# v and u of twelve sample tiles as two blocks of Strassen products, in an encoder layer of 256 + 2048 tokens

## The chip, the cores and the metric

The kernel runs on one core of one Trainium2 chip. The metric is device time in microseconds (us) of one execution. The engines are TensorE (PE, with its weight loads PEld), VectorE (DVE), ScalarE (ACT), GpSimd (POOL) and SyncE (SP). All DMAs of this kernel are issued from SP's queue, in program order.

## The reference

One encoder layer in float32, applied to 256 prompt tokens and, separately, to 2048 sample tokens, with D = 1024.

```python
h = rms_norm(x, g_pre)
q, k, v, z_a, u_f, z_f = jnp.split(h @ w_in, ...)      # six parts of 512 columns
y_a = neighbourhood_attention(q, k, v, rpb)            # grid of 64 columns, 8 heads of 64,
                                                       # window 8 rows x 16 columns, softmax with bias
y_f = fourier_mix(u_f, w_fourier, b_fourier)           # real part of a 2-D FFT (tokens, 64 channels)
                                                       # per group, then a 512x512 product and a bias
mixed = concat([rms_norm(y_a, g_na) * silu(z_a), rms_norm(y_f, g_f) * silu(z_f)])
return x + rms_norm(mixed @ w_out, g_post)
```

## The kernel before

**Products.** Every fp32 product is made of three matmuls of parts in a reduced format (fp32r): an operand a is split in a high part ah (a cast, on ACT) and a low part al = a - ah (on DVE or POOL), and `mm3` adds ah bh, ah bl and al bh in PSUM. Its three lines, L160 to L162, hold most matmuls of the profile; a line there is told apart by its tiles.

**Direct stage (c loop).** Tokens are cut in tiles of 128: c = 0, 1 are the prompt, c = 2 to 17 the 16 sample tiles. For each tile `p_mm` makes v (128 x 512) and then u (128 x 512), 8 k-steps of `mm3` each, from the tile's split x (`x_split`; xh, xl) as stationary operand and the split weights with g_pre multiplied in (wc, `split_w`). The root-mean-square factor comes in when the result leaves PSUM (`v_out`, `u_out`, by invt). `x_square`, `pair_square` and `stats` make it: squares on ACT, sums over k by a reduction on DVE (sq), the sum over partitions by a matmul with ones on PE (pst, L295), then Ln, Exp and a correction. v goes to DRAM in 64 KB pieces (`vD`, with the columns that overlap written twice); each sample tile's u goes right away through the first Fourier step (`u_stage1`, three matmuls into pz), whose result goes to `ZD`. `wo_prep`, one step per tile from c = 8 to 16, loads w_out, splits it and stores it to `woD`.

**Prompt loop (b = 0 to 15).** z, k and q of the prompt, one product of 128 x 256 per step.

**Sample loop (i = 0 to 15).** z, k and q of the samples in Strassen-Winograd form: the k-dimension is halved, tokens are in two groups sg = 0, 1 of 1024 (i < 8 and i >= 8) with two blocks of 512 each, and each i makes two 128-row blocks of output by 7 products of 12 matmuls of 128 x 512. The token operands `bnew[sg, j]` (j = 0 to 6; xh, xl) are sums and differences of scaled x blocks: `n_load`, `n_scale` (x times g_pre times the scale of its token, `inv_all`), `n_sum` (DVE), `n_first` (split) for sg = 0; `n_diff`, `n_put` (to DRAM, `xD`), `b_get`, `b_split` for sg = 1. The weight operands (wa, aop) are made one i ahead: `w_load`, `w_sums` (sums on POOL, L440), `a_split` (ACT and DVE, L454 and L455). The bias tables of attention are made in between (`t_load`, `t_mask`, `t_store`).

**Rest.** Fourier's second stage, attention, output (`po`, L1257), from about 572 us of the span on.

**Order.** Each engine's instructions are in an order written by hand, which is that of the program text. The pool `gp` has 13 buffers of 512 KB (tag g), the pool `hp` 16 of 1 MB (tag k8); in PSUM the tag mm has 5 buffers, b 2, c 1. A tile of a pool waits for the last use of the buffer that it takes.

Of the kernel before, what the change touches and what calls it, by code (L numbers as in the profile page):

```python
# [34 lines left out]
XP = range(4, 17, 3)  # L35
# [88 lines left out]
def layout(inp):  # L124
# [4 lines left out]
    a["xs"] = x[TP:].reshape(32, 4, 16, KC, 128).transpose(2, 4, 3, 1, 0).reshape(16, 128, KC, 128)  # L129
# [3 lines left out]
    a["wv"], a["wu"] = [m.reshape(4, 2, 128, 512).transpose(0, 2, 1, 3) for m in (v, u)]  # L133
# [31 lines left out]
def build(tc, A, O):  # L165
# [13 lines left out]
    uD = dr.tile([TP, 512], F32, name="uD")  # L179
    xD = dr.tile([7, 128, 4, 512], F32, name="xD")  # L180
# [33 lines left out]
    inv_all = hp.tile([128, T], F32, name="inv_all")  # L214
    onesq = hp.tile([128, 128], F32, name="onesq")
    csm = hp.tile([128, 80], F32, name="csm")
    rmask = hp.tile([128, 48], F32, name="rmask")
    nc.gpsimd.memset(onesq, 1.0)
# [33 lines left out]
    def fold_u(raw):  # L252
        t = gt(US, F32, "uc")
# [6 lines left out]
        return t  # L260


    def xload(c):
        xs[c] = load(BS, A["xt"][c] if c < 2 else A["xs"][c - 2], "xr")

    def x_split(c, ks=slice(0, 8)):
        if c not in xh:
# [3 lines left out]
        (nc.gpsimd if c in XP else nc.vector).tensor_tensor(out=l, in0=xs[c][:, ks], in1=h.bitcast(F32),  # L271
                                                            op=ALU.subtract)

    def x_square(c):
        xr = xs.pop(c)
        nc.scalar.activation(xr, xr, AF.Square)
        if c % 2 == 0:
            sqs_[c] = st.tile([128, 256], F32, tag="sq", name="sq")
        nc.vector.tensor_reduce(out=sqs_[c - c % 2][:, c % 2 * 128:c % 2 * 128 + 128],  # L279
                                in_=xr.rearrange("p k t -> p t k"), axis=mybir.AxisListType.X, op=ALU.add)  # L280

    def pair_load(c):
        pr_[c] = k8(F32, "xx", (128, KC, 256))
        for x in range(2):
            nc.sync.dma_start(pr_[c][:, :, 128 * x:128 * x + 128], A["xs"][c - 2 + x])

    def pair_square(c):
        xr = pr_.pop(c)
        nc.scalar.activation(xr, xr, AF.Square)
        sqs_[c] = st.tile([128, 256], F32, tag="sq", name="sq")  # L290
        nc.vector.tensor_reduce(out=sqs_[c], in_=xr.rearrange("p k t -> p t k"), axis=mybir.AxisListType.X, op=ALU.add)

    def stats(c):
# [16 lines left out]
        if c == 0:  # L310
            nc.scalar.copy(inv_all[:, :TP], y)
# [31 lines left out]
    def u_out(g):  # L343
        p = acc.pop(("u", g))
        if pend:
            u_stage1(*pend.pop())
# [212 lines left out]
    for c in range(2):  # L559
        v_out(c)  # L560
# [1025 lines left out]
```

## Time and profile before

| | |
|---|---|
| runs | 1002.38, 1004.58, 1005.26 us; median 1004.58 |
| profiled execution | 1003.15 us, of which the span is 1001.2 us |
| granted TensorE clock, mean | 0.996 |
| matmuls | 5828 |
| bytes moved | 249.33 MB (read 160.13, written 88.08 by memory) |

Stages in the trace, in us of the span: direct stage 5 to 220, prompt loop 220 to 267, sample loop 267 to 572, the rest to 1001. A row of a group reads: line, engine, operation, out<-in, partitions x elements, count | busy us in all, mean ns of one | idle time of the engine before it, and what ended that. A row of the chain or of a timeline begins with start and duration in us. A row of the windows has, behind the stretch, its length and the busy time of PE, PEld, DVE, ACT and POOL with counts, then the granted clock, the DMA share and GB/s. A row of waits has the total, the number and the longest, in us.

### The profile page before, as it was taken

To read this page: it belongs to the slowest core of one execution; us is meant where nothing else is said; L and a number is where in the kernel's file an instruction comes from. 1 tells how busy PE (TensorE), PEld (TensorE's weight loads), DVE (VectorE), ACT (ScalarE), POOL (GpSimd) and SP (SyncE) were. 2 spreads that over 40 slices of the span, in tenths; PEclk is the share of its full clock that TensorE was granted. 3 is DMA by queue.
4 is the path that set the end of the run, shared out by engine and by line. 5 is a ranking of instruction groups with operands and counts; after the bars stand their busy time and mean duration, and the time that the engine had idled before them with its cause. 6 is when DMAs were issued, how large, how long until landed. Compare 5 with 4: busy or idle time off the path is not lost.

```text
span 1001.2 us, 16950 instructions
## 1 busy us (share of the span) xinstructions
PE 987.3 (99%) x5828; PEld 819.9 (82%) x5828; DVE 688.2 (69%) x1295; ACT 474.4 (47%) x1026; POOL 438.3 (44%) x401
## 2 busy tenths in 40 slices
PE   7999999999999999999999999999999999999997
PEld 6778888889988888888888879777787787888886
DVE  7777637668767788697666345776656565648997
ACT  6554424256533322432222255676666665734443
POOL 2300000100336476477657033477577686524444
PEclk9999999999999999999999999999999999999999
DMA  7467788877455685865764898588778799869993
GB/s 257 140 182 222 214 304 310 269 253 255 148 191 194 231 316 191 335 238 210 259 213 169 301 329 298 179 272 286 239 218 260 253 301 295 274 205 343 338 340 129
DMA packets 153253, 249.33 MB, mean 249 GB/s; under 512 B 14032, under 2 KB 99344, under 8 KB 150608
## 3 DMA queue, kind: packets, MB, share of 16 engines
q1 hardware_dynamic: 153168, 248.26, 73.3%
q8 instruction: 46, 0.75, 0.3%
q14 instruction: 39, 0.32, 0.1%
HBM read 160.13 MB, written 88.08 MB: 248 GB/s over the span
## 4 chain that ended last, share of the span: by engine, by line
PE 94%; DVE 2%; DMA 1%; ACT 1%; issue 1%; SPq 0%; POOL 0%; DVEq 0%; ACTq 0%; POOLq 0%
PE po L1257 19%; PE mm L161 17%; PE mm L160 17%; PE mm L162 17%; PE pv L1327 6%; PE ptb L1311 6%; PE s L1006 4%; PE pab L851 2%; DMA wr<-wv 1%; PE py L160 1%; PE py L162 1%; PE py L161 1%; DVE wc L248 1%; DVE sq L279 1%; PE pz L161 0%
## 5 line engine op out<-in xcount | busy, mean ns | idle before, releaser
L161 PE MATMUL mm<-xl,wa 128*128 128x512 f32 x448 | 174.5, 390 | 0.0
L160 PE MATMUL mm<-xh,wa 128*128 128x512 f32 x448 | 174.5, 390 | 0.0
L162 PE MATMUL mm<-xh,wa 128*128 128x512 f32 x448 | 174.5, 389 | 0.0
L160 PE MATMUL mm<-wc,xh 128*128 128x512 f32 x288 | 113.9, 395 | 5.2 <-ACT xh L270 5.2
L161 PE MATMUL mm<-wc,xh 128*128 128x512 f32 x288 | 113.5, 394 | 0.4 <-DVE wc L248 0.3
L162 PE MATMUL mm<-wc,xl 128*128 128x512 f32 x288 | 113.3, 393 | 0.0
L1040 POOL TENSOR_SCALAR w<-w,m 128x480 f32<-128x480 f32 (+6 forms) x136 | 82.0, 616 | 62.2 <-DVE m L1037 48.9
L162 PEld LDWEIGHTS mm<-xh,wa 128*128 128x128 f32 x448 | 84.2, 188 | 17.5
L160 PEld LDWEIGHTS mm<-xh,wa 128*128 128x128 f32 x448 | 84.1, 188 | 17.4
L161 PEld LDWEIGHTS mm<-xl,wa 128*128 128x128 f32 x448 | 84.2, 188 | 17.2
L1257 PE MATMUL po<-wo,yh 128*128 128x512 f32 x272 | 90.4, 413 | 0.0
L1257 PE MATMUL po<-w,yh 128*128 128x512 f32 x280 | 87.6, 395 | 0.0
L1033 ACT ACTIVATE w<-w,m 128x480 f32<-128x480 f32 (+6 forms) x136 | 79.3, 586 | 14.5 <-DVE m L1028 14.5
L455 DVE TENSOR_TENSOR wa<-wr,wa 128x512 fp32r<-128x512 f32 x60 | 63.0, 1057 | 30.0 <-ACT wa L454 29.7
L440 POOL TENSOR_TENSOR ws<-wr 128x512 f32<-128x512 f32 x15 | 24.3, 1622 | 119.2 <-DMA wr<-wz 97.8
L271 POOL TENSOR_TENSOR xl<-xr,xh 128x1024 fp32r<-128x1024 f32 x5 | 12.2, 2450 | 136.0 <-ACT xh L270 125.6
L160 PEld LDWEIGHTS mm<-wc,xh 128*128 128x128 f32 x288 | 54.8, 190 | 16.6 <-ACT xh L270 5.2
L1028 DVE CUSTOM_DVE_ANT_1 w<-s,tb 128x360 f32<-128x360 f32 (+5 forms) x124 | 62.4, 540 | 8.2 <-PE s L1006 7.6
L454 ACT CAST wa<-wr 128x512 fp32r<-128x512 f32 x60 | 36.7, 618 | 65.9 <-issue 25.8
L493 POOL TENSOR_TENSOR mt<-mt,rmask 128x880 f32<-128x880 f32 (+2 forms) x24 | 52.3, 2193 | 33.9 <-DVE mt L489 33.2
L711 DVE TENSOR_TENSOR f<-u,mm 128x512 f32<-128x512 f32 x64 | 43.6, 682 | 32.0 <-PE mm L162 22.3
L161 PEld LDWEIGHTS mm<-wc,xh 128*128 128x128 f32 x288 | 54.8, 190 | 13.2 <-DVE wc L248 1.7
(234 smaller groups left out, 2311.7 us busy)
## 6 DMA issues: line engine op xcount, KB each, us to landing
wr<-wz SPq DMA_DIRECT2D x46, 512.0 KB
oD<-ofs SPq DMA_DIRECT2D x18, 512.0 KB
of<-oD SPq DMA_DIRECT2D x18, 512.0 KB
yr<-yD SPq DMA_DIRECT2D x34, 256.0 KB
woD<-wo SPq DMA_DIRECT2D x16, 512.0 KB
zD<-f SPq DMA_DIRECT2D x16, 512.0 KB
xr<-xs SPq DMA_DIRECT2D x15, 512.0 KB
vD<-vo SPq DMA_DIRECT2D x112, 64.0 KB
```

Source lines behind the costliest of these rows:

```text
L160: nc.tensor.matmul(out, lh, rh, start=first, stop=False)
L161: nc.tensor.matmul(out, lh, rl, start=False, stop=False)
L162: nc.tensor.matmul(out, ll, rh, start=False, stop=last)
L455: nc.vector.tensor_tensor(out=o[:, 1], in0=src, in1=o[:, 0].bitcast(F32), op=ALU.subtract)
L493: nc.gpsimd.tensor_tensor(out=o, in0=i, in1=rmask[:, m0:m0 + n].unsqueeze(2).to_broadcast([128, n, 80]), op=ALU.add)
L711: nc.vector.tensor_tensor(out=dst(f, b), in0=src(uu[u]), in1=src(p), op=op)
L1028: nc.vector.tensor_tensor_reduce(out=rows(g["w"][b][:, h, :n], w), in0=rows(g["s"][2 * b + h][:, :n], w), in1=tv, scale=1.0, scalar=3.0e38 ...
L1033: nc.scalar.activation(w, w, AF.Exp, bias=m[:, h:h + 1], scale=-1.0, accum_out=m[:, 2 + h:3 + h])
L1040: nc.gpsimd.tensor_scalar(w, w, m[:, 4 + h:5 + h], 1.0, ALU.mult, ALU.mult)
L1257: nc.tensor.matmul(p, (d["l"] if x == 2 else d["h"])[:, c], w(n, int(x == 1), c), start=j == 0, stop=j == 11)
L1311: nc.tensor.transpose(ptb[h][:nk, j * 128:j * 128 + 128], g["w"][b][:, h, c0:c0 + nk], ident)
L1327: nc.tensor.matmul(p[hs, b], g["v"][:nk, v, hs], g["pt"][b][:nk, h, j * 128:j * 128 + 128], start=j == 0, stop=j == len(ch) - 1)
```

## The change

NS = 2: only the prompt and four sample tiles (s = 0, 1 of the two blocks b of group 0) keep the direct form (`PL`). For the other twelve, v and u are made as the two output column halves of a Strassen form: `vu` makes, for a group sg and a list S of tile pairs, 7 products per s (j = 0 to 6), each with `bnew[sg, j]` as stationary and a weight operand op_[j] as moving. The seven weight operands are v's and u's halves and sums of them. `r_sum` makes the sums on POOL in the direct stage, `r_put` stores them in DRAM (sD, 5 of 1 MB), `op_load` brings one back, `op_split` splits it on ACT and DVE. `vu(0, range(2, 4))`, 14 products, stands between prompt loop and i = 0; `vu(1, range(4))`, 28 products, between i = 7 and i = 8. In the hooks of the second stand `wo_prep` (one step per product, products 1 to 9), four bias tables (`t_step`), and the weights of i = 8; in those of the first, `n_first`, the last rows for the scales, and the weights of i = 0.

The scales: x is loaded once more by rows (`rows_load`, 9 of 1 MB), ACT squares it with a sum along the row (`rows_square`), `row_scales` makes 1/rms. Where a scale has to lie along the columns, `spread` multiplies the identity by it (ACT, dg, two buffers) and lets ones times dg (fp32, on PE) fill PSUM; `n_scale` then reads it from there.

v and u of the samples go to DRAM by token (`vN`, `uN`, 256 KB a tile); `v_copy` makes vD from vN, DRAM to DRAM, in i = 9 to 11; `u_load`, `u_split`, `u_stage1` follow in i = 8 to 14.

```diff
-    def stats(c):
-        p = ps.tile([128, 256], F32, tag="c", name="pst", bufs=1)
-        nc.tensor.matmul(p, onesq, sqs_.pop(c), start=True, stop=True)
...
+    def rows_square(i):
+        t = xm.pop(i)
         for x in range(2):
+            nc.scalar.activation(t[:, x], t[:, x], AF.Square, accum_out=ssq[:, 2 * i + x:2 * i + x + 1])
...
+    def spread(p, c0, n):
+        for x in range(n):
+            dg = st.tile([128, 128], F32, tag="dg", name="dg")
+            nc.scalar.activation(dg, ident, AF.Copy, scale=invt[:, c0 + x:c0 + x + 1])
+            nc.tensor.matmul(p[:, 128 * x:128 * x + 128], onesq, dg, start=True, stop=True)
...
+    def v_copy(i):
+        x, b, c0, n, d0 = VC[i]
+        nc.sync.dma_start(vD[x][:, d0:d0 + n], vN[b][:, c0:c0 + n])
...
     def n_sum(x):
...
+        if x < 2:
+            for k in range(0, 4, 2):
+                nc.gpsimd.tensor_tensor(out=nq[o][:, k:k + 2], in0=nq[i0][:, k:k + 2], in1=nq[i1][:, k:k + 2],
+                                        op=op)
+        else:
+            nc.vector.tensor_tensor(out=nq[o], in0=nq[i0], in1=nq[i1], op=op)
...
+    def op_load(j):
+        if j < 2:
+            l = [load(US, A["wv"][j][:, 2 * x:2 * x + 2], "vr") for x in range(2)]
+        else:
+            l = [gt(US, F32R, "vl") for x in range(2)]
+            for x in range(2):
+                nc.sync.dma_start(f_(l[x]), sD[(3, 2, 1, 0, 4)[j - 2]][:, 2 * x:2 * x + 2])
+        op_[j] = [None, l]
+
+    def op_split(j):
+        r = op_[j][1]
+        h = op_[j][0] = [gt(US, F32R, "vh"), hp.tile([128, 2, 512], F32R, tag="vw", name="vh", bufs=3)]
...
+    def vu(sg, S, hooks):
+        seq = [(j, s) for j in range(3) for s in S]
+        for x in range(0, len(S), 2):
+            seq += [(j, s) for j in (3, 4, 5) for s in S[x:x + 2]]
+        seq += [(6, s) for s in S]
+        loads, splits = {2: ({0: 2, 2: 3, 4: 4, 6: 5, 8: 6}, {2: 2, 4: 3, 6: 4, 8: 5, 10: 6}),
+                         4: ({0: 2, 4: 3, 8: 4, 10: 5, 16: 6}, {4: 2, 8: 3, 12: 4, 14: 5, 20: 6})}[len(S)]
+        uc, u4 = {}, {}
+        for i, (j, s) in enumerate(seq):
+            if i in loads:
+                op_load(loads[i])
+            if i in splits:
+                op_split(splits[i])
+            for f in hooks.get(i, ()):
+                f()
+            p = mmt(512)
+            h, l = op_[j]
+            th, tl = bnew[sg, j]
+            for k in range(4):
+                mm3(nc, p, th[:, k, 128 * s:128 * s + 128], tl[:, k, 128 * s:128 * s + 128], h[k // 2][:, k % 2],
+                    l[k // 2][:, k % 2], k == 0, k == 3)
...
+                put_rows("v" if j in (1, 6) else "u", sg, int(j in (4, 6)), s, o)
...
+        if 4 <= b < 12:
+            x, y = divmod(b - 4, 2)
+            n_scale(None, *divmod(x, 2)[::-1], range(2 * y, 2 * y + 2))
+        if b in (8, 11):
+            n_first((b - 8) // 3)
+        if b in (12, 13):
+            op_load(b - 12)
         if b > 11:
...
+            n_sum(b - 12)
+        if b in (14, 15):
+            op_split(b - 14)
+        if b == 15:
+            n_first(2)
...
+    e = 7 * (4 - NS)
+    for x in range(4):
+        at((0, 2, 4, 6)[x], n_first, x + 3)
+    for x in range(4):
+        at((1, 3, 6, 8)[x], rows_load, x + 5)
+        at((4, 6, 9, 10)[x], rows_square, x + 5)
+    at(11, row_scales, 10, 8)
+    at(e - 4, w_load, 0)
+    at(e - 2, w_sums, 0)
+    for j in range(6):
+        at(e - 2 + j // 3, a_split, 0, j)
+    vu(0, range(NS, 4), hooks)
     for i in range(16):
         sg, pr = divmod(i, 8)
+        if i == 8:
+            hooks.clear()
+            for x in (5, 6):
+                at(2 * x - 9, b_split, x)
+            for x in range(9):
+                at(x + 1, wo_prep, x)
+            for x in range(28):
+                at(x, t_step, 1 + x // 7, x % 7)
+            at(20, w_load, 8)
+            at(24, w_sums, 8)
+            for j in range(7):
+                at(24 + j // 2, a_split, 8, j)
+            vu(1, range(4), hooks)
...
+            if i == 0 and j == 1:
+                spread_group(1)
...
+            elif i == 7:
+                if j in (3, 4):
+                    op_load(j - 3)
+                if j in (5, 6):
+                    op_split(j - 5)
...
+            if sg:
+                x, y = divmod(7 * pr + j, 3)
+                if x < 16 and y == 0:
+                    u_load(x)
+                if 0 < x < 17 and y == 0:
+                    u_stage1(x - 1)
+                if x < 16 and y == 2:
+                    u_split(x)
+            if 9 <= i < 12 and j in (1, 4):
+                v_copy(2 * i - 18 + j // 4)
```

407 lines of the change are left out of this document (213 added, 194 removed).

## The prediction

> **What bounds the kernel now.** I read the page first (span, busy shares, chain of waits), then PE's waits, PE's timeline in the direct stage, then the windows.
>
> ```profile
> span 1001.2 us, 16950 instructions
> ...
> PE 987.3 (99%) x5828; PEld 819.9 (82%) x5828; DVE 688.2 (69%) x1295; ACT 474.4 (47%) x1026; POOL 438.3 (44%) x401
> ...
> PE 94%; DVE 2%; DMA 1%; ACT 1%; issue 1%; SPq 0%; POOL 0%; DVEq 0%; ACTq 0%; POOLq 0%
> ```
>
> ```profile
> PE mm L160 <- ACT xh L270: 5.2, 1, 5.2
> ...
> PE mm L161 <- DVE wc L248: 0.3, 1, 0.3
> PE pz L161 <- DVE ul L355: 0.3, 1, 0.3
> PE pz L160 <- ACT uh L353: 0.2, 1, 0.2
> ```
>
> TensorE carries 94% of the chain, and behind its first operand (5.2 us) it waits for under a microsecond in any one place. So a matmul that goes is worth its time in full, and every wait that the change brings is added in full: no slack is left on PE to absorb it. What a matmul is worth is not its row's mean:
>
> ```profile
> L160 PE MATMUL mm<-wc,xh 128*128 128x512 f32 x288 | 113.9, 395 | 5.2 <-ACT xh L270 5.2
> ```
>
> ```profile
> 42.14 0.39 PE L160 MATMUL mm<-wc,xh 128*128 128x512 f32 x1
> 42.37 0.39 PE L161 MATMUL mm<-wc,xh 128*128 128x512 f32 x1
> 42.59 0.39 PE L162 MATMUL mm<-wc,xl 128*128 128x512 f32 x1
> 42.82 0.39 PE L160 MATMUL mm<-wc,xh 128*128 128x512 f32 x1
> ```
>
> Each lasts 0.39 us but the next begins 0.227 us later ((42.82-42.14)/3): they overlap, and the pace is 0.227. One product of twelve takes 12 x 0.227 = 2.72 us.
>
> **Part by part: what goes.** v and u now take 18 tiles x 2 x 8 k-steps x 3 = 864 matmuls (three rows of x288). Afterwards there are 6 direct tiles (2 prompt, 4 sample), 288 matmuls, and 14 + 28 products of 12, 504 matmuls: 792. The 72 that go are 72 x 0.227 = -16.3 us (with the row's mean it would be 28, which is wrong). z, k, q and Fourier matmuls stay as many.
>
> The nine sums of squares on PE (pst) go too:
>
> ```profile
> 66.72 0.43 PE pst L295 x2
> ```
>
> 9 x 0.43 = -3.9 us. The small waits in the wait table for wc, ul and uh (0.3 + 0.3 + 0.2) stand in code that is shortened or replaced; I count -0.8.
>
> **The scales by rows.** They are made by ACT's accumulated Square (off PE) and then spread over columns by 18 fp32 matmuls of 128 columns, 10 in the direct stage and 8 at i=0. By half of pst, each is 0.22 us, 3.9 in all. But each needs a diagonal made by ACT, in two buffers:
>
> ```profile
> L308 ACT COPY inv_all<-ry 128x128 f32<-128x128 f32 x16 | 5.2, 427 | 12.7 <-DVE ry L302 12.7
> L680 ACT ACT_TABLE_LOAD x1 | 1.3, 1283 | 0.0
> ```
>
> ```profile
> L471 DVE TENSOR_TENSOR wl<-wr,wh 128x1024 fp32r<-128x1024 f32 x12 | 14.6, 1221 | 5.1 <-ACT wh L470 4.7 <-DMA woD<-wo 0.4
> L402 DVE TENSOR_TENSOR nx<-nx 128x2048 f32<-128x2048 f32 x2 | 4.6, 2288 | 0.0
> ```
>
> ```profile
> L391 POOL TENSOR_TENSOR nx<-nx 128x1024 f32<-128x1024 f32 x8 | 21.2, 2655 | 1.7 <-DMA xD<-nx 1.2
> ```
>
> An ACT pass over 128x128 is 0.427 us, longer than the matmul it feeds, so ACT sets the pace: 18 x 0.427 = +7.7 us (bounds: 3.9 if ACT runs ahead, 10 if each group also waits a microsecond for ACT to clear its evacuation). I take 7.7, the row of the shape.
>
> **Into the first block of products.** The operand sums n_sum(0) and n_sum(1) move to POOL, four of 2.655 us, 10.6 us. They begin at step b=12 of the prompt loop, when the last n_scale is through. On DVE n_sum(2) waits for them, and the split of the first weight operand (two of 1.221) is queued behind it. So the operand is ready 10.6 + 2.3 + 2.4 = 15.3 us after b=12. PE comes there after four prompt steps:
>
> ```profile
> 225.07 0.28 PE L160 MATMUL mm<-ph,wh 128*128 128x256 f32 x1
> 225.19 0.28 PE L161 MATMUL mm<-pl,wh 128*128 128x256 f32 x1
> ```
>
> 24 matmuls, 0.12 us apart, are 2.88 us a step, four are 11.5. PE waits +4 us (0 if POOL starts two steps earlier; 8 if DVE, which must do all n_scale and n_first in the same stretch, is two steps behind).
>
> **The first block** (14 products, 38 us). Its five summed operands come back from DRAM, 1 MB each, among 4 MB of rows and the stores of v and u. All DMAs are issued by SP in program order, and the load of op4 stands behind stores that wait for DVE's sums of products 2 and 3, so it is issued at about product 4, behind the load of op3, for product 8. I count 2 us of wait there, 1 us for op5, nothing for op6. At the end, row_scales sits on ACT ahead of the splits of i=0, with three table changes of 1.28 us, since Ln and Exp stand between passes of other tables: i=0 begins 3.8 us late. Together +7 us (0 when the loads come early and ACT is a stage ahead, 12 when each operand is 2 to 3 us late).
>
> **The second block** (28 products, 76 us) is where most is decided. The preparation of w_out, one step per direct tile of 48 x 0.227 = 10.9 us before, is issued at one step per product of 2.72 us, and four of the bias-table steps come in there too:
>
> ```profile
> woD<-wo SPq DMA_DIRECT2D x16, 512.0 KB
> ...
> mt<-tr SPq DMA_DIRECT2D x8, 600.0 KB
> tD<-mt SPq DMA_DIRECT2D x8, 600.0 KB
> ...
> wr<-wo SPq DMA_DIRECT2D x8, 512.0 KB
> ...
> tD<-mt SPq DMA_DIRECT2D x8, 480.0 KB
> ...
> tD<-mt SPq DMA_DIRECT2D x8, 440.0 KB
> ```
>
> ```profile
> 130.00:140.00 10.00, 10.00 (x46) 8.29 (x45) 4.42 (x9) 4.50 (x8) 0.00 (x0) 1.00 1.01 380
> 420.00:430.00 10.00, 10.00 (x46) 8.29 (x45) 10.00 (x5) 4.90 (x6) 8.40 (x3) 1.00 0.91 302
> ```
>
> (Last columns: granted clock, DMA share, GB/s.) With all engines busy the queues move 380 GB/s. Ahead of op4's load on SP stand, in program order, 12 of the 16 stores and 7 of the 8 loads of w_out (10.0 MB), op2 and op3 (2.1), one bias table in and out and the next one in (0.6 + 0.6 + 0.48 + 0.44 + 0.6 = 2.7), four stores of v (256 KB each by the diff, 1.0): 16 MB, and op4's own 1.05 (two of 128x1024 in fp32). i=7, with its operand loads, leaves some 2 MB. That is 19 MB, 50 us at 380 GB/s. PE needs op4 at product 14, 14 x 2.72 = 38 us after the start of the block. So PE waits 12 us, in one or several pieces (some at op3, product 12), and one more for the split (an ACT pass and a DVE pass of 1.22 on the second half). After that op5 and op6 have the queue to themselves. +13 us. Bounds: 0 if half of the w_out traffic finds room before the block or op4's load does not stand behind it, and 25 at the 302 GB/s of the second row (19/0.302 = 63 us).
>
> The Trainium skill ("DMA: Bandwidth & Descriptors", Specifications) gives about 358 GB/s as the share of one core in the memory's rate. By it the 19 MB would take 53 us, and the wait be 3 us longer; the trace's window at 380 stands above it, so I keep the measured rate.
>
> **Behind it.** In i=9 to 11 v is copied from DRAM to DRAM, 7.3 MB in all, and u comes back tile by tile for 16 stage-one steps that stood in the direct stage before (as many matmuls, so nothing on PE). The stretch of i=8 to 11 is 76 us of PE. I take +1 us (0 to 8: u's loads are asked for only 8 us ahead).
>
> **Sum.** -16.3 - 3.9 - 0.8 + 7.7 + 4 + 7 + 13 + 1 = +11.7 us. The profiled execution took 1003.15 us (1.95 outside its span); it becomes 1014.9, **1015 us**. It lies 1.4 below the median of the runs, 1004.58, and within them.
>
> **Rivals.**
>
> *Faster: the loads arrive in time.* If the second block's DMA wait does not arise, and neither do most of the first's, what counts is PE's own work: -21.0 + 7.7, and 2 us for the entry into the first block. That is 1003.15 - 11.3 = 992 us (987 to 998). The place is the load of op4 in the second block; it decides whether that load lands before 38 us. The point is 38 x 0.38 = 14.4 MB ahead of it: if under that much really is moved by then (w_out loads come before the block, slots free early), nothing is lost. For it speaks that the windows before show room in the sample loop, ahead of the second block:
>
> ```profile
> 300.00:310.00 10.00, 10.00 (x45) 8.28 (x45) 7.49 (x10) 2.39 (x3) 4.56 (x3) 1.00 0.20 78
> ```
>
> Against it: the order of SP's queue puts w_out ahead of op4, whatever room there was earlier. Chance 0.30.
>
> *About the same.* Only the second block's wait is absent, and the others stand: 1014.9 - 13 = 1002 us (999 to 1006). Chance 0.10, of which 0.08 lie within 0.3%.
>
> *Slower still, by transfers.* The second block moves at 302 GB/s, and v's copies collide with u's loads: 12 us more than the forecast, 1027 us. Chance 0.12.
>
> *Slower still, by a clock that falls.* In its first microseconds, behind an idle PE, the matmuls are almost twice as far apart:
>
> ```profile
> 6.22 0.63 PE L162 MATMUL mm<-wc,xl 128*128 128x512 f32 x1
> 6.65 0.63 PE L160 MATMUL mm<-wc,xh 128*128 128x512 f32 x1
> ...
> 10.15 0.63 PE L162 MATMUL mm<-wc,xl 128*128 128x512 f32 x1
> ```
>
> From 5.2 to 10.58 us a dozen matmuls go at 0.43 us, a loss of 12 x 0.2 = 2.4 us. If a wait in the middle of the kernel brings that back, three long waits cost 7 us more: 1022 us. The kernel before has no wait in the middle of over 0.3 us, so no row shows whether it does. The Trainium skill ("TensorE: Matmul & The Clock Gate", section "What's actually happening") says that TensorE falls to half its clock after an idle window of about 3.4 us: by that rule waits of 4 us and more are paid so, and shorter pieces are not. Chance 0.12.
>
> **How the numbers follow.** The forecast itself (1006 to 1020) has 0.36, the two slower cases 0.24, the same 0.10, the faster 0.30. A measurement of this kernel tells about 0.3%, 3 us, from no change. Faster by more than that: 0.30 and 0.02 of the middle case, 0.32; same 0.08; slower 0.60. The range of 8 in 10 leaves out the lower end of the faster case and the worst of the transfers: 988 to 1027. Cases of both signs hold the chance; the forecast's own range is 1006 to 1020.
>
> **What would show it.** In the profile after: PE's count lower by 72 of 128x512, by 9 pst, higher by 18 spreads. PE's starts 0.43 apart in the spreads (0.22: ACT runs ahead). A wait of PE of some 4 us at the first product behind the prompt loop, put down to DVE's split. In the second block, PE waits at products 12 to 17 for splits of op3 to op5, these for DMA from sD, and a window there with a DMA share of 1.0. It is wrong if PE runs through both blocks at 2.72 us a product, or if that DMA share stays under 0.8, or if the wait comes from DVE instead of DMA.

## The result: 9% slower, and the profile after

The changed kernel takes 1097.92 us (median; 1096.31 to 1102.37), the kernel before 1004.47: ratio 1.094, 95% interval 1.0905 to 1.0977. The forecast of 1015 (988 to 1027) had the sign and missed the size by far. The profiled execution took 1098.56 us, its span 1096.7. First the page of the kernel after: span, busy shares, queue and chain.

```profile
span 1096.7 us, 17025 instructions
...
PE 1017.7 (93%) x5774; PEld 821.2 (75%) x5774; DVE 693.6 (63%) x1295; ACT 504.1 (46%) x1085; POOL 459.6 (42%) x412
...
q1 hardware_dynamic: 146960, 277.62, 72.5%
...
PE 71%; DMA 11%; DVE 5%; issue 3%; POOL 3%; SPq 3%; ACT 2%; DVEq 0%; ACTq 0%; POOLq 0%
```

PE has 54 records fewer, as counted: 72 matmuls less, and of the fp32 ones, which have two records each, 9 pst less (18) and 18 spreads more (36). But its part of the chain falls from 94% to 71%, and DMA, DVE, SP's queue and POOL take what it loses. No engine has a larger busy share than before: DVE goes from 69% to 63%. PE's idle time goes from 13.9 to 79.0 us of the span, and its busy time from 987.3 to 1017.7 us although it has less work: most of the time went into waits, the rest into slower matmuls. PE's longest waits (in all, times, longest):

```profile
PE pz L164 <- ACT ut L364: 10.2, 3, 9.7
PE mm L165 <- DVE vl L480: 9.3, 6, 3.3
PE mm L164 <- DVE vuo L507: 8.8, 4, 5.4
PE mm L164 <- DVE uc L507: 5.8, 1, 5.8
PE ivt L312 <- ACT dg L311: 5.7, 1, 5.7
...
PE mm L166 <- DVE wl L568: 3.7, 1, 3.7
```

By stages, first the kernel before (direct stage, prompt loop, sample loop), then after (direct, prompt loop, first block, i=0 to 7, second block, i=8 to 15, the rest). Columns as in the windows before: length, busy times, granted clock, DMA share, GB/s.

```profile
5.21:220.40 215.19, 214.30 (x928) 175.74 (x928) 143.03 (x191) 96.73 (x146) 23.84 (x13) 1.00 0.75 244
220.40:267.16 46.76, 46.76 (x389) 46.63 (x388) 41.33 (x30) 31.14 (x42) 7.31 (x4) 1.00 0.58 188
267.16:571.83 304.67, 304.67 (x1347) 252.45 (x1346) 214.52 (x243) 95.46 (x138) 170.93 (x90) 1.00 0.65 236
```

```profile
5.29:93.54 88.25, 79.61 (x309) 62.40 (x310) 52.98 (x71) 45.25 (x92) 31.61 (x16) 0.92 0.65 228
93.54:149.77 56.23, 49.07 (x385) 47.84 (x384) 38.43 (x33) 27.94 (x37) 14.30 (x4) 0.97 0.80 305
149.77:198.00 48.23, 42.00 (x171) 32.23 (x169) 37.49 (x34) 32.76 (x40) 0.54 (x1) 0.96 0.68 249
198.00:364.44 166.44, 162.03 (x688) 129.50 (x689) 110.73 (x140) 59.20 (x88) 73.55 (x44) 0.98 0.59 219
364.44:477.17 112.73, 88.93 (x337) 67.72 (x336) 64.68 (x57) 30.79 (x32) 39.94 (x17) 0.89 0.80 291
477.17:666.75 189.58, 174.15 (x722) 136.58 (x721) 100.81 (x131) 57.00 (x96) 62.56 (x39) 0.96 0.67 234
666.75:1096.70 429.95, 421.91 (x3171) 344.87 (x3169) 288.06 (x831) 248.69 (x697) 236.64 (x289) 0.99 0.81 267
```

Against what PE needs in each (matmuls by 0.227 us; the prompt loop, half of the sample loop and the rest by the kernel before), with the excess that the prediction's terms stand for:

| stage | PE's need | after | excess | forecast of it |
|---|---|---|---|---|
| direct, 288 matmuls | 65.4 | 88.3 | 22.9 | 8 (ten spreads 4.3; 3.5 that the stage lost before too, 4.3 less the 0.8 of small waits) |
| prompt loop | 46.8 | 56.2 | 9.4 | 4 |
| first block, 168 | 38.1 | 48.2 | 10.1 | 3 |
| i=0 to 7 | 152.3 | 166.4 | 14.1 | 7 (eight spreads 3.4, late start 3.8) |
| second block, 336 | 76.2 | 112.7 | 36.5 | 13 |
| i=8 to 15, with 48 of u | 163.2 | 189.6 | 26.4 | 1 |
| the rest | 429.4 | 430.0 | 0.6 | 0 |

The excess is 120 us where 36 were forecast: the 84 us by which the profiled execution passes 1014.9. No stage ahead of the rest was free of the error, and nearly three fifths of it (49 us) lie in the second block and behind it.

Not all of the excess is waiting. PE's idle time in the six stages (length less busy time) is 66 us. The rest is PE's own time: the spreads, the matmuls at a granted clock of 0.89 to 0.98, and a slower pace at full clock. The kernel after, in the direct stage, in a stretch with a granted clock of 1.00:

```profile
42.08 0.39 PE L164 MATMUL mm<-wc,xh 128*128 128x512 f32 x1
...
42.78 0.39 PE L164 MATMUL mm<-wc,xh 128*128 128x512 f32 x1
```

The second row is three matmuls and 0.70 us behind the first, 0.233 each, where the prediction's rows of the kernel before, at the same place, have 0.227. The sample loop before makes 1344 such matmuls in 304.67 us, 0.2267 each; the last eight i of run e11 (below, no waits, clock 1.00) make 720 in 167.99, 0.2333 each. Over the 2184 matmuls of 128x512 in these stages the difference is 14 us, which is in every changed kernel here and which no moved load brings back. Those of 128x256 keep 0.12. Why the pace differs is not known: no run tests it.

### The profile page after: what moved, and what is told of

It is laid out like the page before. It is cut to its first block, busy times and chain, and to the rows that moved or that the text cites. A ratio compares the mean times of both kernels' runs of the same rounds, so it can differ in the third digit from the quotient of the medians.

```text
span 1096.7 us, 17025 instructions
## 1 busy us (share of the span) xinstructions
PE 1017.7 (93%) x5774; PEld 821.2 (75%) x5774; DVE 693.6 (63%) x1295; ACT 504.1 (46%) x1085; POOL 459.6 (42%) x412
## 4 chain that ended last, share of the span: by engine, by line
PE 71%; DMA 11%; DVE 5%; issue 3%; POOL 3%; SPq 3%; ACT 2%; DVEq 0%; ACTq 0%; POOLq 0%
PE po L1409 17%; PE mm L165 11%; PE mm L166 11%; PE mm L164 11%; PE pv L1479 5%; PE ptb L1463 5%; PE s L1158 4%; DMA wr<-wo 2%; PE pab L1003 2%; DMA mt<-tr 1%; DMA nx<-xq 1%; DMA v<-vD 1%; DMA zD<-f 1%; DMA ut<-uN 1%; POOL mt L587 1%
## 5 line engine op out<-in xcount | busy, mean ns | idle before, releaser
L166 PE MATMUL mm<-xh,wa 128*128 128x512 f32 x448 | 178.9, 399 | 2.8 <-DVE wa L549 2.8
L164 PE MATMUL mm<-xh,wa 128*128 128x512 f32 x448 | 178.0, 397 | 2.0 <-ACT wa L548 2.0
L165 PE MATMUL mm<-xl,wa 128*128 128x512 f32 x448 | 178.9, 399 | 0.0
L164 PE MATMUL mm<-vh,xh 128*128 128x512 f32 x168 | 70.9, 422 | 18.7 <-DVE vuo L507 8.8
L165 PE MATMUL mm<-vl,xh 128*128 128x512 f32 x168 | 71.2, 424 | 9.3 <-DVE vl L480 9.3
L549 DVE TENSOR_TENSOR wa<-wr,wa 128x512 fp32r<-128x512 f32 x60 | 52.8, 886 | 34.1 <-ACT wa L548 34.1
L166 PE MATMUL mm<-vh,xl 128*128 128x512 f32 x168 | 69.7, 415 | 0.0
L1479 PE MATMUL pv<-pt,v 128*64 128x128 f32 (+4 forms) x896 | 62.3, 280 | 0.0
L1479 PEld LDWEIGHTS pv<-pt,v 128*64 128x64 f32 (+4 forms) x896 | 47.4, 135 | 19.0 <-issue 16.3
L1409 PEld LDWEIGHTS po<-w,yh 128*128 128x128 f32 x280 | 52.8, 190 | 11.0 <-issue 0.2
L1463 PE MATMUL ptb<-ident,w 128*128 128x128 f32 (+4 forms) x428 | 60.5, 279 | 0.0
```

The lines of the kernel that those rows point to most:

```text
L164: nc.tensor.matmul(out, lh, rh, start=first, stop=False)
L165: nc.tensor.matmul(out, lh, rl, start=False, stop=False)
L166: nc.tensor.matmul(out, ll, rh, start=False, stop=last)
L549: nc.vector.tensor_tensor(out=o[:, 1], in0=src, in1=o[:, 0].bitcast(F32), op=ALU.subtract)
L1409: nc.tensor.matmul(p, (d["l"] if x == 2 else d["h"])[:, c], w(n, int(x == 1), c), start=j == 0, stop=j == 11)
L1463: nc.tensor.transpose(ptb[h][:nk, j * 128:j * 128 + 128], g["w"][b][:, h, c0:c0 + nk], ident)
```

## The experiments

Medians of four runs each, beside runs of the kernel before on the same chip (1003.8 to 1004.5).

| run | us | against 1097.9 |
|---|---|---|
| e1_fill: waits filled with idle matmuls | 1092.9 | -5.0 |
| e2_wo_early: w_out out of the second block | 1075.2 | -22.7 |
| e3_scales_early | 1089.9 | -8.1 |
| e4_u_ahead | 1096.6 | -1.4 |
| e5_u_t: u earlier, bias tables later | 1096.9 | -1.1 |
| e6_wo_bytes: w_out's DMAs without its passes | 1090.7 | -7.2 |
| e7_block0 | 1094.4 | -3.5 |
| e8_dve_sums | 1095.1 | -2.9 |
| e9_all: e2, e3, e5, e7, e8 and the weights of i=9 early | 1052.0 | -45.9 |
| e10_all_t: e9 with all bias tables late | 1064.2 | -33.7 |
| e11_all_s: e9, spreads and u's splits moved | 1037.4 | -60.5 |
| e12_one_block: e11 without the first block | 1040.0 | -57.9 |

The kernel after itself ran from 1096.3 to 1102.4. The intervals of e1, e4, e5, e7 and e8 (as ratios to the kernel before) overlap its own, so gains of 1 to 5 us are not shown by the times alone.

**Is it the clock?** In the windows the stages with waits show less than full clock (0.89 in the second block). e1 keeps PE busy through eleven of the waits; the edit at eight of them:

```diff
+            keep({(0, 0): 12, (0, 8): 20, (1, 7): 10, (1, 8): 33, (1, 9): 14, (1, 11): 10, (1, 12): 42,
+                  (1, 14): 70}.get((sg, i), 0), f1h, th[:, 0, :256])
             p = mmt(512)
```

> The changed kernel with matmuls that nobody reads (f1h by 256 columns of a token operand, into the spare PSUM bank) put on TensorE ahead of the ten longest waits, as many as fit each wait at 0.12 us: 44 ahead of the first spread, 12 and 20 in the first block, 36 at i=0, 10, 33, 14, 10, 42 and 70 in the second block, 76 ahead of the first u_stage1. The result is the same. Theory A (the half clock behind the waits is a cost of its own, some 25 to 30 us of the 93): the granted clock goes from 0.967 to over 0.99, the records at half clock nearly vanish, and the time falls by 15 to 25 us, to 1073 to 1083 us. Theory B (only the waits count: what PE would gain it waits longer for DMA and DVE): clock up, time within 4 us of 1098, or a few us more where a filling overruns its wait.

The clock of e1, and its second block:

```profile
core 0: 1093.0 us, clock 0.989
```

```profile
361.74:474.16 112.42, 104.71 (x517) 86.76 (x516) 65.41 (x58) 31.46 (x33) 40.40 (x17) 0.97 0.80 293
```

The clock went from 0.967 to 0.989, which is worth some 24 us of PE's time (0.022 x 1096.7, an estimate), and the second block only from 112.7 to 112.4 us. There PE was not what set the time, so a faster PE only waits longer: close to theory B. PE still waits behind most of the fillings (0.5 us ahead of the first spread, 3.0 behind the 42 matmuls in the second block), so they did not take the gain themselves; the 70 at product 14 leave no wait and may overrun by about 1 us. The fall of the clock was mostly a companion of the waits, not a cost of its own; of the 93 us it carries about 5, and even those are not clear of noise.

**The second block.** Its chain, in order of time (start, duration), and SP's queue there:

```profile
375.10 8.65 DMA wr<-wo
...
412.19 7.35 DMA wr<-wo
```

```profile
372.86 0.32 SPq L857 DMA_DIRECT2D qD<-f  x1
...
418.38 0.94 SPq L465 DMA_DIRECT2D vl<-sD  x2
```

```profile
429.75 1.98 ACT L479 CAST vh<-vl 128x1024 fp32r<-128x1024 f32 x2
```

```profile
429.88 1.28 DVE L688 SCALAR_TENSOR_TENSOR wo<-wr,gmix,wo 128x1024 fp32r<-128x1024 f32 x1 [7.20 <-ACT wo L687]
431.08 0.68 DVE L507 TENSOR_TENSOR uc<-uc,mm 128x512 f32<-128x512 f32 x1
```

Each load of w_out takes 5 to 9 us to land (from its issue to ACT's pass). ACT's pass waits for it; DVE's pass waits for ACT; and the next product's sum (vuo, uc) stands behind it on DVE, so its PSUM buffer isn't freed, and PE waits for DVE though a DMA is what is late. op4's load is issued at 418.4 behind these, 54 us into the block, and its split begins at 429.75, 65 us into it; the prediction had it landing at 50, for a product that wants it at 38. So by far the larger part of the delay lies ahead of the issue, in SP's order.

Two experiments: e2 moves the nine steps away and gives them buffers of the tag vw, e6 leaves their DMAs and takes ACT's and DVE's passes out (it stores w_out unscaled, twice).

```diff
-            o = [gt((128, D), F32R, "wo") for y in range(2)]
+            o = [hp.tile([128, D], F32R, tag="vw", name="wo", bufs=3) for y in range(2)]
...
-            for x in range(9):
-                at(x + 1, wo_prep, x)
...
+            if 1 <= i < 7 and (7 * i + j - 7) % 4 == 1 and (7 * i + j - 7) // 4 < 9:
+                wo_prep((7 * i + j - 7) // 4)
```

> The changed kernel with the nine steps of wo_prep moved out of the second block of products into i=1 to 6, one per four products, in the three buffers of the tag vw, which stand empty there. Theory A (the second block waits because w_out's 12.6 MB and its passes stand ahead of the products' sums on DVE and ahead of op3 to op5 in the DMA queues): the block shrinks from 112.7 us to 80 to 88 us, the waits for vuo and uc nearly go, and the time falls by 25 to 32 us, to 1066 to 1073 us. Theory B (the bias tables and the five operands alone fill the queues): the block still takes over 100 us and the time falls by under 12 us. Theory C (what leaves the block comes back as waits in i=1 to 6): the block shrinks and i=0 to 7 grow from 166 us by as much.

```diff
-            o = [gt((128, D), F32R, "wo") for y in range(2)]
-            nc.scalar.activation(o[0], w, AF.Copy, scale=g)
-            nc.vector.scalar_tensor_tensor(out=o[1], in0=w, scalar=g, in1=o[0].bitcast(F32), op0=ALU.mult,
-                                           op1=ALU.subtract)
             for y in range(2):
-                nc.sync.dma_start(woD[hf, y, c], o[y].bitcast(F32))
+                nc.sync.dma_start(woD[hf, y, c], w)
```

> The changed kernel with w_out's split left out: wo_prep in the second block still loads each 512 KB and stores it twice, straight from the loaded tile, so that all its bytes move and SP still waits for each load, but ACT and DVE have nothing to do for it (what is stored is w_out unscaled, twice). Theory A (the bytes ahead of op3 to op5 make the block's wait, as the prediction had it): the block stays at 105 us or more and the time within 6 us of 1098. Theory B (the bytes would fit; what hurts is that each product's sum stands behind w_out's pass on DVE, which waits for ACT, which waits 7 to 8 us for its load, so PSUM's buffers aren't freed): the waits for vuo and uc go, the block falls below 92 us, the time to 1072 to 1080 us.

i=0 to 7 and the second block of e2, then the second block and PE's longest wait of e6:

```profile
199.09:372.95 173.86, 167.73 (x688) 132.83 (x689) 123.69 (x142) 63.41 (x93) 72.94 (x42) 0.95 0.72 271
372.95:456.17 83.22, 80.38 (x337) 64.21 (x336) 59.75 (x54) 26.16 (x27) 40.28 (x17) 0.98 0.72 267
```

```profile
362.50:470.21 107.71, 85.81 (x338) 66.01 (x336) 57.05 (x49) 22.48 (x24) 37.49 (x17) 0.90 0.82 304
```

```profile
PE mm L164 <- ACT vh L479: 13.1, 2, 11.5
```

In e2 the block is 83.2 us, 29.5 less; 7 of these come back in i=0 to 7, where w_out's steps now stand, so theory A holds with some of C. In e6 the waits for sums mostly go, but the block keeps 107.7: the wait becomes a single one of 11.5 us for op4's split. So the bytes and SP's order together carry most of this wait, as the prediction had it, and the queue of passes on ACT and DVE a smaller part (7 us). Bytes and order are not parted here, nor is the share of the buffers that e2 and e6 leave free.

**The spreads' wait.** DVE and POOL of the kernel after, ahead of the first spread:

```profile
64.11 2.26 DVE L305 SCALAR_TENSOR_TENSOR invt<-rt,ry 128x2 f32<-128x2 f32 x1
...
68.90 0.16 DVE L305 SCALAR_TENSOR_TENSOR invt<-rt,ry 128x2 f32<-128x2 f32 x1
```

```profile
59.31 4.75 POOL L452 TENSOR_TENSOR ru<-ru,rv 128x1024 f32<-128x1024 f32 x2 [19.97 <-DMA sD<-ru]
64.02 4.63 POOL L452 TENSOR_TENSOR rv<-rv,ru 128x1024 f32<-128x1024 f32 x2
```

An instruction over two elements a partition takes 2.25 us as long as POOL sums, about one of POOL's four instructions (2.3 us each), and 0.16 as soon as it has ended.

```diff
         if c == 4:
-            for i in (2, 4):
-                rows_square(i)
-                row_scales(2 * i, 2)
...
         vu_out("v", c)
+        if c == 3:
+            for i in (2, 4):
+                rows_square(i)
+                row_scales(2 * i, 2)
```

> The changed kernel with the last two squares and row_scales of the first ten tiles moved ahead from the start of c=4 to between v and u of c=3, so that their small DVE instructions run before POOL's r_sum. Theory A (DVE's instructions of 128x2 elements take 1.3 to 2.3 us instead of 0.16 because POOL's sums of 128x1024 run beside them, and this makes the wait of 5.7 us ahead of the first spread): the small instructions take 0.16 us, the wait falls below 1.5 us, the stretch at half clock behind it becomes shorter, and the time falls by 6 to 10 us, to 1088 to 1092 us. Theory B (the chain of ACT's squares is late whatever POOL does): the wait remains above 4 us, only moved, and the time stays within 3 us of 1098.

1089.9 us, theory A. Three of the small instructions still met POOL's sums, from 60.5 us on; PE's wait ahead of the first spread fell to 1.2 us. The Trainium skill ("GPSIMD Engine Reference", section "1. Specifications") says that POOL shares its SBUF interfaces with VectorE, with contention for DVE instructions in a 2-port perf mode or with two SBUF inputs; the trace agrees for L305, which has two, and shows the price: a tiny instruction waits as long as one of POOL's takes.

**i=8.** PE waits 9.7 us for u's first tile.

```diff
-                if 0 < x < 17 and y == 0:
-                    u_stage1(x - 1)
-                if x < 16 and y == 2:
-                    u_split(x)
+                if 1 < x < 18 and y == 0:
+                    u_stage1(x - 2)
+                if 0 < x < 17 and y == 2:
+                    u_split(x - 1)
```

> The changed kernel with u's tiles asked for two steps (six products) ahead of their u_stage1 instead of one. Theory A (the wait of 9.7 us at i=8 and the small ones behind it are the way of a load of 64 KB pieces from DRAM, asked for 8 us ahead): pz's waits fall from 15 us to under 4, the 13 us at half clock behind the first vanish, and the time falls by 15 to 20 us, to 1078 to 1083 us. Theory B (SP's queue is late at i=8, behind the stores of the second block, so the load comes as late as before and PE waits at the next thing): the time falls by under 6 us.

```diff
+            at(25, u_load, 0)
             vu(1, range(4), hooks)
...
-            if i == 5 or 8 <= i < 11:
-                t_step(max(0, i - 3) if sg else 0, j)
+            if i == 5 or 9 <= i < 12:
+                t_step(max(0, i - 4) if sg else 0, j)
...
-                if x < 16 and y == 0:
-                    u_load(x)
+                if x < 15 and y == 0:
+                    u_load(x + 1)
```

> The changed kernel with u's first tile asked for in the second block (product 25, ahead of the last stores of v), each further one a step (three products) earlier than it was, and the last three bias tables in i=9 to 11 instead of 8 to 10. Asking earlier alone had left the time within 1.5 us, since the wait for ACT became one for DVE, which stood at a bias table. Theory A (at i=8 u's load comes late on SP behind v's last stores, and u's split stands on DVE behind a mask that waits for its table: both have to go): pz's waits fall from 15 us to under 5 and the time by 10 to 17 us, to 1081 to 1088 us. Theory B (the queues are full at i=8 whatever the order, with 4 MB of weights, u and stores): the wait moves to the operands wa, the time falls by under 5 us.

e4: 1096.6, e5: 1096.9 us, theory B both times. In e5 u's first tile was there in time, and the wait went to the second: its split stood on ACT behind splits of the weights of i=9. DVE, SP and ACT of e5:

```profile
477.66 4.29 DVE L552 SCALAR_TENSOR_TENSOR wa<-wr,wa 128x512 fp32r<-128x512 f32 x2
...
483.08 0.68 DVE L507 TENSOR_TENSOR vuo<-u,mm 128x512 f32<-128x512 f32 x1
```

```profile
483.78 0.32 SPq L345 DMA_DIRECT2D vN<-vuo  x1
484.19 1.53 SPq L232 DMA_DIRECT2D wr<-wz  x2
```

```profile
489.54 1.15 ACT L551 ACTIVATE wa<-wr 128x512 fp32r<-128x512 f32 x2 [8.00 <-DMA wr<-wz]
```

The chain reads upward: ACT waits for the weights of i=9; SP asked for them at 484.2, behind the last store of v; this waited for the block's last sum (483.1), which stood on DVE behind splits of i=8's weights, two in 4.3 us beside POOL's masks (0.68 each without POOL).

**The first block.** e7 clears its end, e8 takes POOL out of n_sum.

```diff
-        at((1, 3, 6, 8)[x], rows_load, x + 5)
-        at((4, 6, 9, 10)[x], rows_square, x + 5)
-    at(11, row_scales, 10, 8)
-    at(e - 4, w_load, 0)
+        if x == 3:
+            at(8, w_load, 0)
+        at((1, 3, 6, 10)[x], rows_load, x + 5)
+        if x < 3:
+            at((4, 6, 9)[x], rows_square, x + 5)
...
                 if i == 0 and j == 1:
-                    spread_group(1)
+                    rows_square(8)
+                if i == 0 and j == 2:
+                    row_scales(10, 8)
...
                         n_load(x)
+                        if x == 0:
+                            spread_group(1)
```

> The changed kernel with the last square of rows, its row_scales (with the table loads) and the second spreads moved from the end of the first block into i=0 and i=1, and the weights of i=0 asked for two products earlier, ahead of the last rows. Theory A (i=0 begins late because its splits stand on ACT behind squares, two table loads and late weights): the waits for wa (2.0 and 2.8 us) and the stretch at half clock at 198 us go, and the time falls by 6 to 10 us, to 1088 to 1092 us. Theory B (the same work only stands in the way one i later): the time falls by under 3 us.

```diff
-        if x < 2:
-            for k in range(0, 4, 2):
-                nc.gpsimd.tensor_tensor(out=nq[o][:, k:k + 2], in0=nq[i0][:, k:k + 2], in1=nq[i1][:, k:k + 2],
-                                        op=op)
-        else:
-            nc.vector.tensor_tensor(out=nq[o], in0=nq[i0], in1=nq[i1], op=op)
+        nc.vector.tensor_tensor(out=nq[o], in0=nq[i0], in1=nq[i1], op=op)
```

> The changed kernel with n_sum(0) and n_sum(1) back on DVE (two of 128x2048) instead of four of 128x1024 on POOL. Theory A (the sums on POOL cost DVE more than they take from it: beside them the two splits of the prompt weights take 6.7 us instead of 2.8, POOL's own sums 3.6 us instead of 2.65, and PE waits 3.7 us for the split): the wait for wl L568 goes, the first product of the block begins 3 to 6 us earlier, and the time falls by 3 to 6 us. Theory B (DVE is full in that stretch, so that 4.6 us more on it delay the first operand by as much as POOL did): within 2 us of 1098.

e7: 1094.4 us; the waits for wa go, but the spreads, moved to the start of i=1, now wait themselves, behind silu and evacuations on ACT:

```profile
PE iv L312 <- ACT dg L311: 5.7, 1, 5.7
```

So at most half of theory A's gain, for theory B's reason. e8: 1095.1 us, at the least gain that theory A allows, with an interval that doesn't part it from theory B by itself. Its mechanism is in the trace of the kernel after: beside POOL's sums (3.8 us each instead of 2.65) DVE's two splits took 6.7 us; in e8 they take 1.22 each again and the wait for wl falls from 3.7 to 0.9 us, while that for the block's first operand grows from 1.5 to 2.5:

```profile
139.24 6.70 DVE L568 SCALAR_TENSOR_TENSOR wl<-wr,wh 128x1024 fp32r<-128x1024 f32 x2
```

```profile
133.90 7.64 POOL L422 TENSOR_TENSOR nt<-nx 128x1024 f32<-128x1024 f32 x2 [65.24 <-DVE nx L397]
```

**All together.**

e9 joins the edits of e2, e3, e5, e7 and e8, and adds:

```diff
-                if j in (0, 3):
+                if j == 3 or i == 0 and j == 0:
                     w_load(i + 1 + j // 3)
...
+            at(24, w_load, 9)
```

> The changed kernel with the single repairs together: w_out's steps in i=1 to 6, the scales of c=3 early, the end of the first block cleared, n_sum on DVE, u's loads and the last bias tables moved, and the weights of i=9 asked for at product 24 of the second block instead of behind v's last stores. Theory A (each wait has a cause of its own, and i=8 waits since SP reaches the weights of i=9 only when DVE has made the block's last sums): the single gains add up (23, 8, 3, 3) and i=8 gives 10 more: 1047 to 1058 us. Theory B (the waits are one backlog of DVE and DMA work that turns up at the next place): the gain stays under 32 us, 1066 us or more.

e10 adds to e9:

```diff
-            for x in range(28):
-                at(x, t_step, 1 + x // 7, x % 7)
...
-            if i == 5 or 9 <= i < 12:
-                t_step(max(0, i - 4) if sg else 0, j)
+            if i == 5 or 9 <= i:
+                t_step(max(0, i - 8) if sg else 0, j)
...
-            dg = st.tile([128, 128], F32, tag="dg", name="dg")
+            dg = st.tile([128, 128], F32, tag="dg", name="dg", bufs=5)
```

> The kernel of the run before, with the four bias tables taken out of the second block too (one per i in i=9 to 15, as many bytes as before there), and five buffers instead of two for the diagonals of the spreads. Theory A (what is left of the block's waits comes from the tables' 8.7 MB and POOL's masks beside DVE's splits, and the spreads are paced by ACT and PE taking turns): the block goes to under 79 us, the two groups of spreads from 0.6 to under 0.45 us each, and the time falls by 5 to 10 us against the run before. Theory B (the block's rest and the spreads are set by something else, the operands' splits and fp32 on TensorE): within 3 us of it.

e9: 1052.0 us, theory A. Five single gains add to 38.3 (22.7, 8.1, 1.1, 3.5, 2.9; the last three not clear of noise); the other 7.6 came with the weights of i=9 asked for at product 24, which wasn't run alone. i=8 to 15 take 176 us in e9 (441.8 to 618.0 in its span) against 189.6 after and 190.4 in e2, where w_out's steps were gone from the block and this edit was missing: so their waits were not a backlog of those steps. e10: 1064.2, 12 us slower, against both theories. Its spreads did gain, as theory A had it: ten in 2.9 us (65.26 to 68.19 in its span) instead of 4.4 in e9 (65.30 to 69.73), so with two buffers for dg ACT and PE take turns. The second block is 80.9 us instead of 83.3, but the rest of the kernel takes 445 us instead of 428. The start of Fourier's second stage in e9, and in e10:

```profile
620.00:640.00 20.00, 20.00 (x237) 18.09 (x239) 11.20 (x34) 10.49 (x29) 1.41 (x1) 1.00 0.88 316
```

```profile
620.00:640.00 20.00, 16.36 (x131) 15.98 (x130) 5.80 (x22) 5.38 (x12) 0.00 (x0) 0.58 1.02 384
```

The DMA share is 1.02 there and the granted clock 0.58 (0.74 in the next 20 us), while PE's waits of over 0.7 us in this part are one of 3.6 us (for abl): by these two windows the clock costs some 14 us (20 x 0.42 + 20 x 0.26, an estimate): here a slow PE seems to carry most of the loss. Why the clock stayed down so long, and whether the late tables' transfers are behind it, was not tested.

e11 adds to e9:

```diff
-                        if x == 0:
-                            spread_group(1)
...
+            if i == 1 and j == 1:
+                spread_group(1)
...
-                if x < 16 and y == 2:
+                if x < 16 and y == 1:
                     u_split(x)
```

> The run with all single repairs, with the second group of spreads put at product 1 of i=1 (behind no evacuation and no silu on ACT) instead of product 0, and u's splits one product earlier. Theory A (the wait of 5.6 us ahead of these spreads and the 5.5 us of waits for ut are places in ACT's and DVE's order): both fall below 2 us, the stretch at half clock behind the spreads goes, and the time falls by 7 to 12 us against 1052, to 1040 to 1045 us. Theory B (ACT and DVE are behind anyway there): within 3 us of 1052.

e12 is e11 with:

```diff
-NS = 2
+NS = 4
...
+        if c == 6:
+            for x in range(4):
+                n_load(divmod(x, 2)[::-1])
+        if c in (7, 8):
+            for x in range(2 * (c - 7), 2 * (c - 7) + 2):
+                n_scale(None, *divmod(x, 2)[::-1])
+        if c == last:
+            for x in range(4):
+                n_sum(x)
...
+        if b in (0, 2, 4, 6, 8, 10):
+            n_first(b // 2)
...
-    vu(0, range(NS, 4), hooks)
```

> One part alone: the kernel of the run before (e11) with only the second block. The four further sample tiles of the first group are made directly, the first block of 14 products is gone, x blocks and scales of group 0 are loaded and made in the direct stage, the rest (rows of the second group, its scales, the weights of i=0) in the prompt loop. There are 24 matmuls more, 5.4 us. Theory A (the first block, with its five operands from DRAM and the work crowded into the prompt loop ahead of it, costs more than its 24 matmuls save): prompt loop at 47 to 49 us instead of 52, no waits there nor at i=0, and the time falls by 8 to 15 us against e11. Theory B (the same work makes the same waits in the direct stage): within 4 us of e11, or above it.

In e12 two of group 0's seven operands are split after the sums that change their sources instead of ahead of them, so they hold other values; instructions are the same in number and kind. i=8 to 15 of e11, then the direct stage of e12:

```profile
436.81:604.80 167.99, 167.99 (x721) 135.14 (x720) 103.65 (x131) 57.06 (x98) 64.41 (x39) 1.00 0.71 257
```

```profile
5.26:129.44 124.18, 120.37 (x500) 95.47 (x501) 77.19 (x95) 54.08 (x104) 32.73 (x16) 0.99 0.70 256
```

e11: 1037.4 us, below theory A's range; i=8 to 15 now needs 168.0 us with PE busy throughout, and the 4.8 above 163.2 are the slower pace alone (720 x 0.0066). e12: 1040.0; its interval (1.0335 to 1.0384) overlaps e11's (1.0315 to 1.0372): theory B. The direct stage of e12 has 480 matmuls, 109 us, and takes 124.2, an excess of 15; its prompt loop takes 56.4. The first block saves 24 matmuls, 5.4 us, and spends them: with it or without, in these two placings, it is the same time.

So 60 of the 93 us went by other places for the same work (and other buffers and engines for parts of it). The best version is still 3.4% slower than the kernel before (interval 3.2 to 3.7%), and none was found that beats it. What is left in e11 by stages, against PE's need: direct 13.0, prompt loop 5.1, first block 9.0, i=0 to 7 17.7, second block 8.0, i=8 to 15 4.8: 57.6 us, where 24.5 are earned (16.3 of matmuls, 3.9 of pst, and the 4.3 that the direct stage lost before). 14 of the 57.6 are the slower pace. Which of the others could go by better placing stays open.

## Why the prediction was wrong

- **What goes** was right in count: 5774 records fit, and the price of a matmul is its pace, not the row's 0.39. The 0.8 us of small waits did not go: those for wc alone became 2.7 us (two, 34 to 37 us into the span).
- **What stays** was not in the sum: the prediction let the matmuls that remain keep 0.227 us. They run at 0.233, 14 us in all. Why stays open.
- **The spreads'** price was near: ten in 6.0 us (68.96 to 74.95), eight in 3.5, 9.5 against 7.7. What failed is the step before them: that they are fed in time. The prediction priced dg by ACT's row and didn't ask when the scales are there. PE waited 5.7 us for them, 8.1 with what followed (e3). This term wasn't in the sum.
- **Into the first block**, +4: the prompt loop's excess was 9.4. POOL's sums were taken at 2.655 us and DVE beside them at full speed; they were 3.4 to 3.8 and DVE's splits 3.35. PE's wait came earlier than forecast, at the prompt's own weights (wl L568, 3.7 us), and only 1.5 us at the first operand. Four waits for wl L565 (3.4 us) were in no term; e8 leaves 3.2 of them, and their cause was not followed. The kernel before showed the price beside the row that the prediction used: POOL's sums of 128x1024 run there from 314.3 to 325.2 us, and a split of DVE that takes 0.69 us without them takes

```profile
314.98 2.28 DVE L455 TENSOR_TENSOR wa<-ws,wa 128x512 fp32r<-128x512 f32 x1
```

- **The first block**, +7 with its end: its waits were near, 4.2 us for operands where 3 were given, and 4.8 for the weights wa of i=0 where 3.8 were. What the excess of 10.1 and of i=0 to 7 holds beyond them is PE's own time (42.0 us busy instead of 38.1 in the block), pace and clock.
- **The second block**, +13, is the term with the right mechanism and the wrong size: 36.5. The 16 MB ahead of op4 were counted well, but moved at 380 GB/s from the first microsecond. In the trace SP stands at a store of q until 372.9, 8 us into the block, and each w_out step then waits for its own load of 5 to 9 us, so the queue wasn't full: the block moved 291 GB/s on average. The lower bound of 302 that the prediction quoted was the nearer one. And the waits for sums, on DVE behind w_out's passes, were not seen as a way in which the same bytes stop PE earlier.
- **Behind it**, +1, was 26.4. This is the largest failure of a step: the stage was priced by bytes alone. SP's order (weights behind stores behind sums) was not followed past the block's end, though the prediction had followed it inside. With the edits of e9 and e11, which change this order and that of u's splits, the stage falls by 21.6 us (189.6 to 168.0); the other 4.8 are pace.
- **The rivals.** Transfers at 302 GB/s (1027) came nearest, and not near. The clock was a rival of 7 us and is about 5: near in size by luck, since it fell behind many more than three waits (0.967 over the span, 36 us of PE's time), and cost little because PE was waiting there anyway. By the Trainium skill ("TensorE: Matmul & The Clock Gate", section "What's actually happening") the clock falls behind an idle window of about 3.4 us. Here it fell already behind two waits of 0.8 and 1.8 us, 34.4 and 37.2 us into the span (the kernel after: PE's two waits, and the window around them, clock 0.94; the matmuls from 38.1 to 41.1 us start 0.43 us apart), so shorter pieces are paid too, against what the prediction said of them.

```profile
34.37 0.49 PE L165 MATMUL mm<-wc,xh 128*128 128x512 f32 x1 [0.83 <-DVE wc L255]
37.16 0.50 PE L165 MATMUL mm<-wc,xh 128*128 128x512 f32 x1 [1.82 <-DVE wc L255]
20.00:40.00 20.00, 17.35 (x70) 13.30 (x69) 19.18 (x13) 13.32 (x30) 19.34 (x10) 0.94 0.58 191
```

- **The signs** that the prediction named came out mixed. PE's counts fit. Ten spreads take 6.0 us behind their wait, at half clock, and 4.4 in e3, where the wait is short: 0.44 each, as forecast. In the second block PE waits for splits of operands (7.8 us), but as much and more for DVE's sums (vuo 8.8, uc 5.8): the case that the prediction called a sign of being wrong. Behind those sums stand w_out's loads, so DVE is where the wait shows and not its cause.
- **What is common** to these: each stage was given one wait, worked out from one resource, with all other queues taken to be on time. Here four in-order queues hand delays to each other, so terms that were summed as separate each start late, and the range, made of separate bounds, was far too narrow.

## What to carry to other kernels

When a kernel has PE at 99%, removed matmuls count in full, but so does every place where the added work puts a DMA, a pass and a sum into one queue: follow each added load from its issue through every in-order queue to the instruction of PE that needs it, and do so past the end of the changed stage. Preparation for later stages belongs where queues are empty, not beside work that PE waits for: moving nine steps, with buffers of their own, took off 23 us without removing one byte. A wait that is put down to an engine with little to do (vuo on DVE) can have its cause behind that engine's previous instruction. And before an excess is put down to waits, compare the pace of the matmuls that the change left alone.

## What the runs showed of the hardware that was not expected

- A DVE instruction over 128x2 elements takes 2.25 us beside POOL sums of 128x1024 and 0.16 us without them; splits of 128x1024 take 3.35 instead of 1.22.
- The granted clock falls behind short waits that come close together (0.8 and 1.8 us), and where PE is kept busy through the waits it stays up (0.989 against 0.967); it brings 5 us at most where DMA sets the time.
- A load of 512 KB takes 5 to 9 us to land in the second block, where the queues hold many others.
- At a granted clock of 1.00 and without waits, the same matmuls of 128x512 start 0.227 us apart in the kernel before and 0.233 in every changed kernel; those of 128x256 keep 0.12. The cause is not known.
